# Seven block products for the mixer's last projection, memory's keys and values ahead of it, and the small-tile pool given up where the recurrences end

## The chip, the cores and the metric

The kernel runs on one core of a Trainium2 chip. Its time is the device time of one execution in microseconds; the median of several runs counts. Beside the times there is a profile of one execution: when each instruction of each engine started and how long it took, what released it when it had waited, and what the DMA queues moved. The engines are TensorE (PE in the profile; PEld is its weight load), VectorE (DVE), ScalarE (ACT), GpSimd (POOL) and SyncE (SP), which here issues DMAs.

## The reference

One layer of a streaming encoder is applied to 512 prompt tokens and 64 sample tokens, D_MODEL 1024, all in float32. After an input projection come two linear-attention recurrences in chunks of 64 tokens; their outputs are gated, projected and merged, and the merged rows go through `w_o`. That last projection, the cross-attention's keys and values and the down-projection are what the change concerns.

```python
# _mixer, its end
y_a = o_a.reshape(B, L, VA).astype(h.dtype) @ p['w_out_a'][l]
y_b = o_b.reshape(B, L, VB).astype(h.dtype) @ p['w_out_b'][l]
merged = jax.nn.sigmoid(gt_a) * y_a + jax.nn.sigmoid(gt_b) * y_b
return merged @ p['w_o'][l], conv_new, s_a_new, s_b_new

# _trunk, for the one layer (prompt and sample each)
x = x + y                                       # y = _mixer(_rmsnorm(x, norm_mix), ...)
x = x + _cross_attn(_rmsnorm(x, p['norm_mem'][l]), mem_k[l], mem_v[l], p['w_mq'][l], p['w_mo'][l])
f, f_new = _conv_ffn(_rmsnorm(x, p['norm_ffn'][l]), ...)
x = x + f                                       # then the final _rmsnorm

# keys and values of the prompt's 256 memory tokens
m = _rmsnorm(mem, g)
return (m @ w_k).reshape(B, M, MEM_HEADS, MEM_HD), (m @ w_v).reshape(B, M, MEM_HEADS, MEM_HD)

# _conv_ffn: 1024 -> 2 x 2816, causal convolution of width 3, gate, then back to 1024
return (jax.nn.silu(gate) * val) @ w_down, new
```

## The kernel before

**Layout.** Features lie on the 128 partitions, tokens in the free dimension: `x` is eight tiles of 128 x 576 (512 prompt tokens, then 64 sample tokens). A projection makes one output tile of 128 features at a time, out of eight blocks of 128 input features. Every float32 product is made of three: weight and operand are each split into a high part of type float32r and the rest, and high x high, high x low and low x high are added up in PSUM. `mm3` and `proj` (lines 621 to 653) write them out; a tile's 576 columns are done as 256 and 320, in the two banks of one `big` PSUM tile, of which there are two. Four `sm` tiles of one bank each serve the rest.

**Stages.** `main` (line 1356) goes through: the input projection's tiles with the recurrences strung in between (`c_gdn`, `c_gla`); 16 gate tiles; the `out` tiles that merge the two branches; `wo`, the last projection of the mixer, which adds into `x` and prepares the next norm (`res_finish`); then for each of four heads the memory's keys (`mk`), for every second head the values (`mv`), and the queries (`mq`), with the attention (`c_att`) strung in; the output tiles `mo`; and the FFN, whose order is written out in `ffn_order` (line 103): 22 times an up-projection pair `up`, and the down-projection in four parts of 6, 6, 6 and 4 blocks.

**Block products.** The down-projection already uses seven products in place of eight. Two output tiles are a pair, two input blocks are an even and an odd one, and the 576 tokens are two halves `N1` and `N2` of 288: a 2 x 2 by 2 x 2 block product, done with seven products of sums (P1, P2, P3, Q4 to Q7). The operand sums are `tu` and `tw` (`operands`, line 1683), the weight sums are `ws` (`emit_product`, line 515). `products` (line 1705) runs through pairs in the order of `product_order` (line 92). In a pair P1, Q6, Q7 and Q4 add up in one bank, Q5 and P3 in a second, P2 has a third; after each product VectorE adds the bank into half a tile of `x`. So a product that adds into a bank waits until VectorE has read it for the product before. All three banks were `sm` tiles.

**Weights.** `WORDER` is the one list in which weights are used. A weight is loaded by SP into one of `RAWB` = 3 raw tiles, then split by ScalarE into tiles of a ring: `WB` = 6, and in the FFN `WF` = 6 more. A projection's weight takes two tiles (high, low), a product's takes one of which it uses the two halves. `fetch` (line 562) prepares weights ahead as long as the ring has room. For most weights the low part is made by ScalarE writing the negated high part and a DMA from the POOL queue that adds the float32 weight onto it (`split_summed`, line 508).

**What sets the order.** All instructions go through `Driver` (line 196), which keeps a planned time for each engine and each tile and issues an instruction at its planned place; chains of small work (`drv.spawn`) fill in between the matmuls of `main`. TensorE's order is the order in which `main` and the chains call it. At run time each engine takes its instructions in that order and waits on semaphores only. Working tiles of 128 x 584 come from a ring of `NS` = 57 slots. Small tiles of the recurrences live in the pool `tp`; at the FFN's start it is closed and `fp`, with the six further weight tiles, takes its place:

```python
drv.flush(float("inf"))
tctx.close()
nonlocal tp, fp
tp = fp = ctx.enter_context(tc.tile_pool(name="fp", bufs=WF))
```

Of the kernel before, what the change touches and what calls it, by code (L numbers as in the profile page):

```python
# [10 lines left out]
F32 = mybir.dt.float32  # L11
# [6 lines left out]
P = 128  # L18
D = 1024
TP = 512  # L20
TS = 64
# [6 lines left out]
NS = 57  # L28
RAWB = 3
WB = 6  # L30
WF = 6
# [17 lines left out]
M_ID, M_TRI, M_NEG, M_N1, M_ONE, M_GLA, M_SH, M_LEV = 0, 128, 256, 384, 512, 640, 768, 896  # L49
# [12 lines left out]
def weight_order():  # L62
    seq = list(HEADS)
    for m in range(8):
        seq += [("gta", m), ("gtb", m)]
    seq += [("out", m) for m in range(8)]
    seq += [("wo", m) for m in range(8)]
    for hd in range(4):
        seq += [("mk", 2 * hd), ("mk", 2 * hd + 1)]
        if hd % 2 == 0:  # L70
            seq += [("mv", 2 * hd + i) for i in range(4)]
        seq += [("mq", 2 * hd), ("mq", 2 * hd + 1)]
    seq += [("mo", m) for m in range(8)]
    for kd, i in FFN:
        if kd == "up":
            seq += [("up", i), ("up", NJ + i)]
        elif kd == "dns":
            seq += [("dn*", u) for u in product_order(i)]
        else:
            seq += [("dn", (m, 3)) for m in i]  # L80
    return seq
# [6 lines left out]

PRODUCTS = ("P1", "Q5", "Q6", "P2", "P3", "Q7", "Q4")


def product_order(pairs):

    seq = []
    for i, pair in enumerate(pairs):
        seq += [(pair, "P1"), (pair, "Q5")]
        if i:
            seq.append((pairs[i - 1], "Q4"))
        seq += [(pair, p) for p in ("Q6", "P2", "P3", "Q7")]
    return seq + [(pairs[-1], "Q4")]  # L100


def ffn_order():
    seq, late = [], []
    for p, js in enumerate(PARTS):
# [4 lines left out]
        late = [("dns", [(m, p) for m in range(0, 8, 2)])]  # L110
    return seq + [("dn", (0, 1)), ("dns", [(2, 3), (4, 3)]), ("dn", (6, 7))]
# [4 lines left out]
WFULL = [w for w in WORDER if w[0] not in ("dn", "dn*")]  # L116
# [79 lines left out]
class Driver:  # L196
# [32 lines left out]
    def where(self, ap):  # L229
# [4 lines left out]
        if ap.space == bass.MemoryType.PSUM:  # L234
            return ap.tensor.name, (0, P, 0, 1024)
# [20 lines left out]
    def rotate(self, tag, bufs, tile_):  # L256
# [3 lines left out]
        if len(q) >= bufs:  # L260
            end, old = self.free_at(tag)
            q.remove(old)
# [151 lines left out]
def tile_trunk(ctx, tc, xT, memT, wt, wd, vec, cst, w0, wgate, st_gdn, st_conv, st_gla, st_ffn, ckT, cv,  # L414
# [57 lines left out]
    def raw_tile():  # L472
        return keep(drv.rotate("raw", RAWB, wp.tile([P, 1024], F32, tag="raw", name=nm("wr"), bufs=RAWB)))
# [11 lines left out]
    def emit_weight(i):  # L485
        kind, idx = WORDER[i]
        if kind == "dn*":
# [25 lines left out]
    halves_of = {}  # L513

    def emit_product(pair, prod):

        m, p = pair
        n = len(PARTS[p]) * 64
        if prod == "P1":
            r = halves_of[pair] = []  # L520
            for i in range(2):
                raw = raw_tile()
                c0 = PART0[p] * 128
                src = wd[m + i, :, c0:c0 + 2 * n]
# [5 lines left out]
        def total(a, b):  # L530
            s_ = slot("ws")
            V.tensor_tensor(s_[:, 0:n], a, b, op=ALU.add)
            r.append(s_[:, 0:n])
            return s_[:, 0:n]

        src = {"P1": lambda: a11, "Q5": lambda: total(a21, a22), "Q6": lambda: total(r[4], a11), "P3": lambda: total(r[5], a12),
               "Q7": lambda: total(a11, a21), "P2": lambda: a12, "Q4": lambda: a22}[prod]()
# [7 lines left out]
        if prod in ("P2", "Q4"):  # L545
            drop(src)
# [15 lines left out]
    def fetch(i):  # L562

        room = WB + (WF if fp is not None else 0)
        for j in range(i, len(WORDER)):
            if j in wready:
                continue
            if len(drv.pending & wnames) + (1 if WORDER[j][0] == "dn*" else 2) > room:
                break
# [11 lines left out]
    cst_t = cp.tile([P, NM], F32, name="cst")  # L581
# [12 lines left out]
    w0_t = cp.tile([P, 256], F32, name="w0")  # L594
    DMA(w0_t, w0)
    ident = cst_t[:, M_ID:M_ID + 128]
    tri = cst_t[:, M_TRI:M_TRI + 128]
    neg = cst_t[:, M_NEG:M_NEG + 128]
    negm1 = cst_t[:, M_N1:M_N1 + 128]
    ones = cst_t[:, M_ONE:M_ONE + 128]  # L600
    shift = cst_t[:, M_SH:M_SH + 128]
    glam = cst_t[:, M_GLA:M_GLA + 128]
# [8 lines left out]
    wg_t = cp.tile([P, 256], F32, name="wg")  # L611
    cst_in = cp.tile([P, 12, 3], F32, name="cstin")
    cst_out = cp.tile([P, 12, 6], F32, name="cstout")
    csamp = cp.tile([P, 12, TS], F32, name="csamp")
# [124 lines left out]
    sg = cp.tile([P, 12, 20], F32, name="sg")  # L739
# [16 lines left out]
    def c_gates(ba):  # L756
        G.memset(bt, 0.0)
        p1 = sm()
        sel = cst_t[:, M_SEL:M_SEL + 8]
# [145 lines left out]
    def c_gdn(h):  # L905
# [118 lines left out]
        for li, b in enumerate(LEVELS):  # L1024
# [10 lines left out]
            lm = cst_t[:, M_LEV + 128 * li:M_LEV + 128 * li + 128]  # L1035
# [318 lines left out]


    def main():
# [53 lines left out]
        DMA(cst_t, cst)  # L1410
# [85 lines left out]
        mem_prep()  # L1496
        yield tuple([("oa", h) for h in range(5)] + [("ob", p) for p in range(2)])
        osx = xs_of(list(zip(oh, ol)))
        mg = []
        for m in range(8):  # L1500
# [8 lines left out]
            h, lo = slot("mgh", F32R), slot("mgl", F32R)  # L1509
            A.copy(h[:, 0:T], g0[:, 0:T])  # L1510
            X.tensor_tensor(lo[:, 0:T], g0[:, 0:T], f(h[:, 0:T]), op=ALU.subtract)
            mg.append((h, lo))

        def res_finish(ps, m, scale, gcol, acc_, out):
            for xx, i in zip(two(x[m]), pv(ps)):
                V.scalar_tensor_tensor(xx, i, scale, xx, op0=ALU.mult, op1=ALU.add)
            out.append(norm_prep(x[m], vcol(gcol + m)))
            sq_acc(acc_, x[m], m == 0)

        acc = slot("acc")  # L1520
        out = []
        for m in range(8):
            xt = slot("x")
            DMA(xt[:, 0:T], xT[:, m, :])
            x[m] = xt
            b = []
            yield from tile_proj("wo", m, xs_of(mg), b)
            res_finish(b[0], m, 0.5, C_GMEM, acc, out)
        xs = xs_of(out)
        drv.spawn(c_rstat("n2", [(acc, 0)], 4, True, 2.0))  # L1530

        first = True
        yield ("nm",)
        N["mrt"], N["mbc"] = N["nm"]
        for hd in range(4):
            kr = slot("kraw")
            for j in range(2):
                wh, wl = weight("mk", 2 * hd + j)
                ps = big()
                for k in range(KT):  # L1540
                    a, b = N["mx"][k]
                    mm3([(ps[:, 0, 0:256], slice(0, 256))], wh, wl, a, b, k, k == 0, k == 7)
                    if k % 2:
                        yield 0.7
                V.tensor_tensor(kr[:, 256 * j:256 * j + 256], ps[:, 0, 0:256], N["mbc"][:, 0:256], op=ALU.mult)
            DMO(o_mk[256 * hd:256 * hd + 256, :].rearrange("(j p) t -> p j t", p=P), r4(kr[:, 0:512], 256))
            N["k", hd] = split(kr)
            ckr, cvr = slot("ckr"), slot("cvr")
            DMA(r4(ckr[:, 0:512], 256), ckT[:, 2 * hd:2 * hd + 2, :])
            DMA(r4(cvr[:, 0:512], 256), cv[:, 256 * hd:256 * hd + 256].rearrange("(a p) d -> p a d", p=P))  # L1550
            N["ks", hd], N["vs", hd] = split(ckr), cvr
            if hd % 2 == 0:
                nh = hd // 2
                vr = [slot("vraw") for _ in range(2)]
                ps = big()
                for kp in range(4):
                    wh, wl = weight("mv", nh * 4 + kp)
                    for tt in range(2):
                        c = slice(128 * tt, 128 * tt + 128)
                        for k in range(2):  # L1560
                            a, b = N["mx"][2 * kp + k]
# [427 lines left out]
```

## Time and profile before

| what | value |
|---|---|
| median of 3 runs | 1142.08 us (1141.47 to 1143.43) |
| the profiled execution | 1141.34 us, span 1139.5 us |
| TensorE busy | 1117.0 us, 8453 matmuls |
| VectorE busy | 628.7 us |
| ScalarE busy | 618.3 us |
| GpSimd busy | 294.8 us |
| HBM read / written | 163.13 MB / 5.37 MB |

A matmul's row lasts some 0.3 us, but the next one starts 0.13 us later: they are pipelined, so a matmul's cost is the distance between starts. The instructions are recorded by one helper, which is why almost all of them carry the same line, L227; they are told apart by the names of their tiles: `big<-xh,w` is a matmul into a `big` tile with operand `xh` and weight `w`. In the rows of the timeline the numbers are start and length, and in brackets at the end the idle time of the engine before it and what ended it. In the rows of stretches the numbers are the length, then for TensorE, its weight loads, VectorE, ScalarE and GpSimd the busy time and the count of instructions, then the granted clock of TensorE (1.00 is full), the mean busy share of the DMA engines and the GB/s they moved.

### The profile page before, as it was taken

Reading aid. Unit: us, or ns where it says so; the run is one execution under the profiler, and the core shown is the slowest. Engines: PE = TensorE matmul, PEld = TensorE weight load, DVE = VectorE, ACT = ScalarE, POOL = GpSimd, SP = SyncE. Lnnn points to the kernel's source line nnn. Section 1 sums busy time; section 2 is a strip of 40 time slices with the busy share of each in tenths; the row PEclk is TensorE's granted clock in tenths of the full one; section 3 lists DMA queues with packets and bytes.
Section 4 is the critical chain, followed back from the end, with each engine's and each line's share of the span. In section 5 each row is a group of like instructions: output and inputs, shape, how many; then the busy total and the mean of one; then the engine's idle time right before and its main releaser. Section 6 shows DMA issues by size and latency. Waiting matters only on the chain.

```text
span 1139.5 us, 21399 instructions
## 1 busy us (share of the span) xinstructions
PE 1117.0 (98%) x8453; PEld 1076.4 (94%) x8453; DVE 628.7 (55%) x1296; ACT 618.3 (54%) x1138; POOL 294.8 (26%) x540
## 2 busy tenths in 40 slices
PE   8999999999999999999999999899999999999997
PEld 7899989998889999999999999899999999999987
DVE  6777646555533135345563443467835773677475
ACT  6766437554534354454545555654646555656554
POOL 4244114521311131111001011324423342343332
PEclk9999999999999999999999999999999999999999
DMA  8665334654336678885836846974697579848834
GB/s 259 149 144 126 63 79 89 153 121 101 80 65 166 173 171 199 224 178 141 230 120 156 205 110 156 230 181 74 141 257 178 100 165 224 208 73 189 189 68 122
DMA packets 61557, 172.53 MB, mean 151 GB/s; under 512 B 7056, under 2 KB 19600, under 8 KB 61456
## 3 DMA queue, kind: packets, MB, share of 16 engines
q0 software_dynamic: 25632, 73.41, 37.8%
q1 hardware_dynamic: 35824, 97.74, 26.2%
q8 instruction: 67, 1.10, 0.4%
q14 instruction: 34, 0.28, 0.1%
HBM read 163.13 MB, written 5.37 MB: 148 GB/s over the span
## 4 chain that ended last, share of the span: by engine, by line
PE 93%; DVE 3%; ACT 2%; DMA 1%; issue 0%; SPq 0%; POOL 0%; ACTq 0%
PE big L227 70%; PE sm L227 22%; DMA wr<-wt 1%; ACT w L227 1%; DVE x L227 1%; DVE fc L227 0%; DVE c L227 0%; SPq L227 0%; ACT xh L227 0%; DVE acl L227 0%; ACT sq L227 0%; DVE xl L227 0%; DVE gy L227 0%; DVE w L227 0%; DVE gna L227 0%
## 5 line engine op out<-in xcount | busy, mean ns | idle before, releaser
L227 PE MATMUL big<-xh,w 128*128 128x256 f32 (+1 forms) x3072 | 554.8, 300 | 6.7 <-DMA wr<-wt 3.9
L227 PEld LDWEIGHTS big<-xh,w 128*128 128x128 f32 x3072 | 463.1, 189 | 13.1 <-issue 8.8
L227 PE MATMUL big<-xl,w 128*128 128x256 f32 (+1 forms) x1536 | 330.3, 297 | 1.8 <-DVE xl L227 1.8
L227 PEld LDWEIGHTS big<-xl,w 128*128 128x128 f32 x1536 | 259.2, 190 | 2.4 <-DVE xl L227 2.4
L227 POOL DMA_DIRECT2D w<-wt x118 | 103.3, 882 | 445.4 <-ACT w L227 411.9
L227 ACT ACTIVATE w<-wr 128x1024 fp32r<-128x1024 f32 (+3 forms) x164 | 148.6, 906 | 109.8 <-PE big L227 52.9
L227 ACT CAST w<-wr 128x1024 fp32r<-128x1024 f32 (+3 forms) x184 | 164.3, 894 | 42.7 <-issue 21.4
L227 PE MATMUL sm<-ach,w 128*128 128x288 f32 (+1 forms) x496 | 103.4, 297 | 5.4 <-DVE x L227 5.4
L227 PEld LDWEIGHTS sm<-ach,w 128*128 128x128 f32 x496 | 80.9, 188 | 7.5 <-DVE x L227 6.7
L227 DVE TENSOR_TENSOR fu<-big,rbc 128x512 f32<-128x512 f32 x88 | 36.2, 454 | 92.4 <-PE big L227 84.0
L227 DVE SCALAR_TENSOR_TENSOR fc<-fu,vec,fc 128x578 f32<-128x578 f32 x88 | 71.1, 818 | 9.7 <-ACT fc L227 9.3
L227 ACT ACTIVATE fc<-fu,vec 128x578 f32<-128x578 f32 x44 | 38.2, 871 | 68.3 <-DVE fu L227 68.3
L227 PE MATMUL sm<-acl,w 128*128 128x288 f32 (+1 forms) x248 | 68.4, 295 | 0.0
L227 POOL COPY fout<-fu 128x2 f32<-128x2 f32 x88 | 34.9, 427 | 123.4 <-DVE fu L227 123.2
L227 DVE TENSOR_TENSOR x<-x,sm 128x288 f32<-128x288 f32 (+1 forms) x100 | 43.7, 449 | 30.0 <-PE sm L227 29.8
L227 POOL DMA_DIRECT2D w<-wd x46 | 40.9, 915 | 69.0 <-ACT w L227 68.9
L227 PEld LDWEIGHTS sm<-acl,w 128*128 128x128 f32 x248 | 46.7, 188 | 0.0
L227 PE MATMUL big<-aoh,w 128*128 128x256 f32 (+1 forms) x256 | 45.1, 296 | 0.0
L227 PE MATMUL big<-oh,w 128*128 128x256 f32 (+1 forms) x256 | 44.9, 296 | 0.0
L227 PE MATMUL big<-mgh,w 128*128 128x256 f32 (+1 forms) x256 | 44.6, 295 | 0.0
L227 PEld LDWEIGHTS big<-oh,w 128*128 128x128 f32 x256 | 38.5, 188 | 0.3 <-DMA w<-wt 0.3
L227 PEld LDWEIGHTS big<-mgh,w 128*128 128x128 f32 x256 | 38.7, 189 | 0.0
(331 smaller groups left out, 1770.6 us busy)
## 6 DMA issues: line engine op xcount, KB each, us to landing
wr<-wt SPq DMA_DIRECT2D x134, 512.0 KB, 5.7
w<-wt POOLq DMA_DIRECT2D x118, 512.0 KB, 7.2
wr<-wd SPq DMA_DIRECT2D x24, 384.0 KB, 3.6
w<-wd POOLq DMA_DIRECT2D x36, 192.0 KB, 4.2
x<-xT SPq DMA_DIRECT2D x16, 288.0 KB, 6.1
w<-ws POOLq DMA_DIRECT2D x12, 192.0 KB, 4.0
wr<-wd SPq DMA_DIRECT2D x8, 256.0 KB, 3.0
o_y<-yo SPq DMA_DIRECT2D x8, 256.0 KB, 3.0
```

Source lines behind the costliest of these rows:

```text
L227: fn(*args, **kw)
```

## The change

1. **Seven products for `wo`.** The eight output tiles become four pairs, the eight input blocks four even-odd pairs. The merged tiles are no longer split as they are (`mgh`, `mgl`); for each second one a chain (`c_wo_operands`) makes the sums and their splits. `products` becomes general: the two banks a and b are now the two banks of one `big` tile, only P2's c is an `sm` tile. The order is the one of the FFN's calls (item 4), in which a pair's Q4 comes after the next pair's Q5; a second order, `whole`, is written and not used. `wo_finish` adds each product into `x`, scaled; `c_norm` prepares the norm after that.
2. **The order of the attention's front** is the list `ATT`: keys of head 0 and the first values, then `wo`, then the second values and keys 1, then queries and the remaining keys. The cached keys and values of the sample tokens are loaded with the queries.
3. **The pool swap** happens where the recurrences end, ahead of the `out` tiles. `fp` now holds three weight tiles (`WF` = 3), a fourth raw tile (`RF` = 1) and the eight tiles of `x` (`xslot`), which are loaded together after the `out` tiles; `NS` is 55. Constants that only the recurrences use move to the small-tile pool, and the constant table is loaded as two parts.
4. **The FFN's products.** The last pair of a call runs P1, Q5, Q6, P3, Q7, P2, Q4 instead of ending in P2, P3, Q7, Q4. The last pair of part 2 moves behind the last up-projection, ahead of the down tiles 0 and 1.
5. **Bookkeeping.** The planner tells PSUM banks apart (`where`); sums of weights are kept by name and a raw tile is given up when all its uses are made; `wo`'s weights are stored with even blocks first.

```diff
-NS = 57
+NS = 55
 RAWB = 3
 WB = 6
-WF = 6
+WF = 3
+RF = 1
...
-PRODUCTS = ("P1", "Q5", "Q6", "P2", "P3", "Q7", "Q4")
...
+def product_order(pairs, whole=False):
     seq = []
     for i, pair in enumerate(pairs):
-        seq += [(pair, "P1"), (pair, "Q5")]
+        last = i == len(pairs) - 1
+        now = [(pair, p) for p in (("P1", "P2", "Q5", "Q6", "Q7") if whole else
+                                   ("P1", "Q5", "Q6", "P3", "Q7", "P2", "Q4") if last else ("P1", "Q5", "Q6", "P2", "P3", "Q7"))]
         if i:
-            seq.append((pairs[i - 1], "Q4"))
-        seq += [(pair, p) for p in ("Q6", "P2", "P3", "Q7")]
-    return seq + [(pairs[-1], "Q4")]
+            now.insert(2, (pairs[i - 1], "Q4"))
+            if whole:
+                now.insert(5, (pairs[i - 1], "P3"))
+        seq += now
+    return seq + ([(pairs[-1], "P3"), (pairs[-1], "Q4")] if whole else [])
+
+WPAIRS = [(("wo", m), ("wo", m + 1)) for m in range(0, 8, 2)]
+
+ATT = [("mk", 0), ("mv", 0), ("wo", 0), ("mv", 1), ("mk", 1), ("mq", 0), ("mq", 1), ("mk", 2), ("mq", 2), ("mk", 3), ("mq", 3)]
...
-        late = [("dns", [(m, p) for m in range(0, 8, 2)])]
-    return seq + [("dn", (0, 1)), ("dns", [(2, 3), (4, 3)]), ("dn", (6, 7))]
+        pairs = [(("dn", (m, p)), ("dn", (m + 1, p))) for m in range(0, 8, 2)]
+        late = [("dns", pairs if p < 2 else pairs[:3])]
+        if p == 3:
+            seq.append(("dns", [(("dn", (6, 2)), ("dn", (7, 2)))]))
+    return seq + [("dn", (0, 1)), ("dns", [(("dn", (m, 3)), ("dn", (m + 1, 3))) for m in (2, 4)]), ("dn", (6, 7))]
...
     def raw_tile():
+        if fp is not None and (len(drv.ring.get("rawf", ())) < RF or drv.free_at("rawf") < drv.free_at("raw")):
+            return keep(drv.rotate("rawf", RF, fp.tile([P, 1024], F32, tag="rawf", name=nm("wr"), bufs=RF)))
...
+    def operands(ce, co, new=None, fe=None, fo=None):
+        u, w = slot("tu"), slot("tw")
+        V.tensor_tensor(u[:, N2], co[:, N2], ce[:, N2], op=ALU.subtract)
+        yield [u]
+        V.tensor_tensor(u[:, N1], ce[:, N1], ce[:, N2], op=ALU.subtract)
+        yield [u]
+        V.scalar_tensor_tensor(w[:, N1], u[:, N2], -1.0, ce[:, N1], op0=ALU.mult, op1=ALU.subtract)
+        yield [w]
+        V.scalar_tensor_tensor(w[:, N2], w[:, N1], -1.0, co[:, N1], op0=ALU.mult, op1=ALU.subtract)
+        if fe is None:
+            fe = hl(ce[:, N1], new)
+            yield [fe[1]]
+            fo = hl2(co, new)
+            yield [fo[1]]
+        fu = hl2(u, new)
+        yield [fu[1]]
+        fw = hl2(w, new)
...
+    def products(pairs, ops, finish, whole=False):
+        ab, cc = {}, {}
+        for pair, prod in product_order(pairs, whole):
+            if prod == "P1":
+                ab[pair] = big()
+            if prod == "P2":
+                cc[pair] = sm()
+            a, b = ab[pair][:, 0, 0:HT], ab[pair][:, 1, 0:HT]
+            c = cc[pair][:, 0:HT] if pair in cc else None
+            o = b if prod in ("Q5", "P3") else c if prod == "P2" else a
+            start = prod in ("P1", "Q5", "P2")
...
+    def swap_pools():
+        nonlocal tp, fp
+        tctx.close()
+        tp = fp = ctx.enter_context(tc.tile_pool(name="fp", bufs=WF))
+
+    def xslot(i, s="x"):
+        return drv.rotate(f"F{i}", 1, fp.tile([P, SLOT], F32R if s != "x" else F32, tag=f"F{i}", name=nm(s), bufs=1))
...
         yield tuple([("oa", h) for h in range(5)] + [("ob", p) for p in range(2)])
+        swap_pools()
...
-            h, lo = slot("mgh", F32R), slot("mgl", F32R)
-            A.copy(h[:, 0:T], g0[:, 0:T])
-            X.tensor_tensor(lo[:, 0:T], g0[:, 0:T], f(h[:, 0:T]), op=ALU.subtract)
-            mg.append((h, lo))
+            if m % 2:
+                drv.spawn(c_wo_operands(m, gates[2 * m - 2], g0))
...
+        mem_prep()
+        for m in range(8):
+            yield from out_tile(m)
+        for m in range(8):
+            x[m] = xslot(m)
+            DMA(x[m][:, 0:T], xT[:, m, :])
...
-        for m in range(8):
-            xt = slot("x")
-            DMA(xt[:, 0:T], xT[:, m, :])
-            x[m] = xt
-            b = []
-            yield from tile_proj("wo", m, xs_of(mg), b)
-            res_finish(b[0], m, 0.5, C_GMEM, acc, out)
...
+        def wo_finish(pair, prod, a, b, c):
+            m = pair[0][1]
+            xx, scale = (x[m], 0.5) if prod in ("P1", "Q6", "P3", "P2") else (x[m + 1], -0.5)
+            half = N1 if prod in ("P1", "P2", "Q4") else N2
+            V.scalar_tensor_tensor(xx[:, half], b if prod in ("Q5", "P3") else c if prod == "P2" else a, scale, xx[:, half],
+                                   op0=ALU.mult, op1=ALU.add)
+            if prod == ("P2" if m == 6 else "P3"):
+                drv.spawn(c_norm(m, C_GMEM, acc, out))
+            elif prod == "Q4":
+                drv.spawn(c_norm(m + 1, C_GMEM, acc, out))
+
+        def c_norm(m, gcol, acc_, out_):
+            yield [x[m]]
+            sq_acc(acc_, x[m], m == 0)
+            drv.done.add(("sq", m))
+            if drv.ready(*(("sq", i) for i in range(8))):
+                drv.spawn(c_rstat("n2", [(acc_, 0)], 4, True, 2.0))
+            while not drv.ready("wo"):
+                yield WAIT
+            out_.append((m, norm_prep(x[m], vcol(gcol + m))))
+            drv.done.add(("norm", gcol, m))
+
+        for kd, i in ATT:
+            if kd == "mk":
+                yield from mem_keys(i)
+            elif kd == "mv":
+                yield from mem_values(i)
+            elif kd == "wo":
+                yield tuple(("wops", m) for m in range(1, 8, 2))
+                yield from products(WPAIRS, [wops[m] for m in range(1, 8, 2)], wo_finish)
+                drv.done.add("wo")
...
-        drv.flush(float("inf"))
-        tctx.close()
-        nonlocal tp, fp
-        tp = fp = ctx.enter_context(tc.tile_pool(name="fp", bufs=WF))
```

345 lines of the change are left out of this document (173 added, 172 removed).

## The prediction

> **What bounds the kernel now.** I read the page's busy shares first, then the chain that ended last, then the waits of TensorE, then the timeline at each of those waits.
>
> ```profile
> span 1139.5 us, 21399 instructions
> PE 1117.0 (98%) x8453; PEld 1076.4 (94%) x8453; DVE 628.7 (55%) x1296; ACT 618.3 (54%) x1138; POOL 294.8 (26%) x540
> PE 93%; DVE 3%; ACT 2%; DMA 1%; issue 0%; SPq 0%; POOL 0%; ACTq 0%
> ```
>
> TensorE is busy for 98% of the span and holds 93% of the chain. Its whole idle time is 1139.5 - 1117.0 = 22.5 us, so time moves in two ways alone: fewer matmuls, or a wait of TensorE that goes or comes. The waits:
>
> ```profile
> PE sm L227 <- DVE x L227: 5.4, 9, 1.8
> PE big L227 <- DMA wr<-wt: 3.9, 1, 3.9
> PE big L227 <- DVE xl L227: 1.8, 2, 1.6
> PE big L227 <- DVE u L227: 1.7, 1, 1.7
> ```
>
> The first two are in the change's reach; the last two lie in the first 50 us, whose order of matmuls stays. The first is bank reuse among the block products (a product adds into a bank that VectorE must first have read); the second is one weight that was late.
>
> **Part 1: the products.** The last projection had 8 tiles x 8 blocks x 3 splits x 2 halves = 384 matmuls; seven products over four pairs are 4 x 7 x 4 x 3 = 336 of 288 columns, so 48 go. Their price:
>
> ```profile
> L227 PE MATMUL big<-mgh,w x256: 275/298/317, 470.9 to 521.7; 128*128 128x256 f32 x128
> 521.86 0.28 PE L227 MATMUL big<-mh,w 128*128 128x256 f32 x1
> 440.00:480.00 40.00, 40.00 (x304) 40.00 (x303) 19.04 (x37) 18.06 (x22) 6.04 (x7) 1.00 0.84 199
> 810.00:834.00 24.00, 24.00 (x183) 24.00 (x183) 15.67 (x36) 14.23 (x25) 9.73 (x14) 1.00 0.91 211
> ```
>
> The stage runs from 470.9 to 521.86, where memory's first key matmul starts: 50.96 / 384 = 0.1327 us each (256 and 320 columns in turn). The two windows' columns are engine busy time and count: 40.00 / 304 = 0.1316 us in the projections, 24.00 / 183 = 0.1311 us in the FFN's existing products of 288 columns, so the new shape costs no more each. 48 x 0.1327 = **-6.4 us**, on TensorE and so on the path.
>
> What the products add elsewhere, in a stage of 336 x 0.1327 = 44.6 us:
>
> ```profile
> L227 DVE TENSOR_TENSOR ws<-ws,wr 128x384 f32<-128x384 f32 x24 | 13.3, 552 | 0.1
> L227 DVE TENSOR_TENSOR aol<-sm,aoh 128x512 fp32r<-128x512 f32 x8 | 5.5, 692 | 22.0 <-ACT aoh L227 22.0
> L227 DVE TENSOR_TENSOR x<-x,sm 128x288 f32<-128x288 f32 x98 | 43.1, 451 | 30.0 <-PE sm L227 29.8
> L227 DVE TENSOR_TENSOR acc<-acc,sq 128x576 f32<-128x576 f32 x23 | 17.3, 754 | 1.4 <-ACT sq L227 1.0
> L227 ACT CAST w<-wr 128x512 fp32r<-128x512 f32 x8 | 4.9, 610 | 0.6 <-DMA wr<-wt 0.5
> ```
>
> VectorE: 16 weight sums and 12 low parts of 512 columns at 0.69 (between the 0.552 of 384 columns and 0.754 of 576; the row of that width says 0.692), 28 adds into x at 0.45, seven square sums at 0.75: 11.0 + 8.3 + 12.6 + 5.3 = 37.2 us, 83% of the stage, against 65% (15.67 of 24.00) in the FFN's products. ScalarE: 28 casts and 16 negated copies at 0.61, 26.8 us or 60%, and eight squares on top. Both fit, so they cost nothing as throughput; what is dear is lateness, next.
>
> ```profile
> 834.67 0.56 PE L227 MATMUL sm<-ach,w 128*128 128x288 f32 x3
> 835.77 0.40 PE L227 MATMUL sm<-ach,w 128*128 128x288 f32 x1 [0.55 <-DVE x L227]
> 807.61 0.40 PE L227 MATMUL sm<-ach,w 128*128 128x288 f32 x1 [0.40 <-DVE x L227]
> ```
>
> At 834.67 the third matmul starts 2 x 0.13 later, 834.93; the next was due at 835.06 and came at 835.77, and its successor follows 0.24 instead of 0.13 behind. A product right behind another in its bank thus loses 0.82 us: the idle figure of 0.55 plus 0.27 of refilling. In the new stage none stands so. The closest distance is one product of 12 matmuls, 1.58 us, for Q6 behind P1 in the first pair and all through the last; elsewhere two or more lie between. Against it stand 0.84 (0.71 + 0.13) plus whatever is ahead on VectorE: at 807.61, in a call's first pair, even two products between did not do, and 0.7 was lost (0.58 late, 0.11 refilling). Bounds: 0 if VectorE is free each time, 0.82 for each of the 28 products, 23 us, if never. I take one such wait in the first pair, where VectorE still makes the last operands, and 0.3 in the last: **+1.0**, near the lower end because the FFN's 98 products, most of them shorter (9 matmuls, 1.18 us), met only nine waits.
>
> **Part 2: the pool swap.** Before, small tiles gave way to six weight tiles at the FFN's start:
>
> ```profile
> 724.46 0.51 PE L227 MATMUL big<-xh,w 128*128 128x256 f32 x2 [3.91 <-DMA wr<-wt]
> 720.00:730.00 10.00, 6.09 (x35) 5.88 (x34) 5.83 (x11) 7.07 (x10) 2.41 (x9) 0.83 1.05 274
> 725.00:730.00 5.00, 5.00 (x28) 5.00 (x27) 4.28 (x7) 3.83 (x6) 1.12 (x5) 0.66 1.05 274
> 800.00:840.00 40.00, 39.05 (x294) 38.59 (x293) 26.21 (x57) 23.75 (x41) 14.28 (x20) 1.00 0.82 190
> ```
>
> The DMA engines are full (1.05), the weight comes late, TensorE idles 3.91 us and then runs at a granted clock of 0.66 for five microseconds. In ten microseconds 35 matmuls were done where the 304-in-40 rate does 76: 41 x 0.132 = **-5.4 us** if the wait goes. I take all of it: after the change up to four weights instead of three stand ready there, and no pool changes hands. [...]
>
> The swap now comes where the recurrences end. TensorE's instruction order is the same up to the last output matmul, with weights for two output tiles, 12.7 us of work, already loaded; x is fetched there in eight loads. Nothing at the swap costs TensorE in my sum; if the cover is gone, it is the 5.4 again (a rival).
>
> **Part 3: the order of the FFN's products.** The last pair of each call now puts P2 between Q7 and Q4, one product of 1.18 us against 0.84. Three calls lost 0.82 and the last 0.91 (1118.53 for a matmul due at 1117.73, plus 0.11):
>
> ```profile
> 1117.47 0.42 PE L227 MATMUL sm<-ach,w 128*128 128x288 f32 x2
> 1118.53 0.38 PE L227 MATMUL sm<-ach,w 128*128 128x288 f32 x1 [0.64 <-DVE x L227]
> ```
>
> 3 x 0.82 + 0.91 = **-3.4**. The first pair's wait at 807.61 (0.7, three times) keeps its order: 0. At the FFN's end one pair of part 2, 63 matmuls or 8.3 us, now stands between the last up-projection and the down tiles 0 and 1, which waited for it:
>
> ```profile
> 1102.65 0.53 PE L227 MATMUL big<-ach,w 128*128 128x256 f32 x2 [0.40 <-ACT ach L227]
> 1103.44 0.54 PE L227 MATMUL big<-acl,w 128*128 128x256 f32 x2 [0.26 <-DVE acl L227]
> 1106.19 0.43 PE L227 MATMUL sm<-ach,w 128*128 128x288 f32 x2
> 1108.39 0.40 PE L227 MATMUL sm<-ach,w 128*128 128x288 f32 x1 [1.77 <-DVE x L227]
> 1110.47 0.41 PE L227 MATMUL sm<-ach,w 128*128 128x288 f32 x1 [0.22 <-DVE x L227]
> ```
>
> The first two lost about 1.0 (their idle time and 0.2 of refilling each); 1108.39 was due at 1106.45 (1.94 + 0.11), 1110.47 lost 0.5: 3.5 in all. But VectorE does the last gate's work while that pair asks for its reads one product apart: I put two waits of 0.7 there, and 0.4 for products that now take a bank pair that the down tiles use just before. -3.5 + 1.4 + 0.4 = **-1.7**; bounds -3.5 and +2.
>
> **Part 4: memory's keys and values.** The same matmuls in another order. The first keys and values cover the making of the last operands; the second pair covers the norm (eight VectorE steps of 0.92 behind eight of ScalarE):
>
> ```profile
> L227 DVE SCALAR_TENSOR_TENSOR xl<-x,vec,xh 128x576 fp32r<-128x576 f32 x24 | 21.8, 920 | 16.1 <-ACT xh L227 16.1
> 531.75 0.39 PE L227 MATMUL big<-w,mh 128*128 128x512 f32 x1
> 540.87 0.42 PE L227 MATMUL big<-xh,w 128*128 128x256 f32 x2
> ```
>
> One call of each lasts from 521.86 to 540.87, 19.0 us with the few matmuls strung in (a value's matmul stands at 531.75), against 7.4 us of norm steps: 0, and a late statistic would cost at most the 1 to 2 us between them and the chain's end.
>
> **Weights.** Nine weight tiles instead of twelve in the FFN. Before, the rows of one late-prepared product:
>
> ```profile
> 806.58 1.75 POOL L227 DMA_DIRECT2D w<-wd  x2 [2.45 <-ACT w L227]
> 818.41 0.30 PE L227 MATMUL sm<-hl,w 128*128 128x288 f32 x1
> w<-wd POOLq DMA_DIRECT2D x36, 192.0 KB, 4.2
> ```
>
> Issued by 808.3 at the latest and landed 4.2 later, 812.5, for use at 818.41: 5.9 us in hand. Three tiles fewer take 3 x 1.18 = 3.5, and 2.4 are left: 0.
>
> **The sum.** -6.4 + 1.0 - 5.4 - 3.4 - 1.7 = -15.9 against the profiled execution's 1141.34, which stands 0.7 below the median of 1142.08: 1125.4 there, 1126 as a median.
>
> **Rivals.**
>
> ```profile
> x<-xT SPq DMA_DIRECT2D x16, 288.0 KB, 6.1
> mem<-memT SPq DMA_DIRECT2D x4, 256.0 KB, 8.7
> ```
>
> (a) *The late weight moves along with the swap*: memory's four loads and x's eight, 1.0 and 2.3 MB, meet the weights, and TensorE waits once behind the swap. For it: the full DMA engines at 720. Against: 12.7 us of weights in hand. 5.4 is given back: 1131.5. (b) *VectorE's lateness takes the products' gain*: at 83% it makes half of the 28 products wait 0.82, 11.5 instead of my 1.0: 1136.5. For it: waits at 807 with VectorE fully packed; against: VectorE stood idle 29.8 us ahead of the 98 adds quoted above, waiting for TensorE. (c) *Slower: nine tiles are too few.* If the 5.9 us in hand are not typical, the four of seven products whose low part is completed by a POOL-issued transfer come late, 48 of the FFN's 84; each by 0.33 us eats the 15.9, and by 0.5 us it is 24: 1150. For it: 2.4 us is thin; against: no weight was late in those stages. [...] Here such a transfer still landed in 4.2 us with VectorE at 65%, so I give it little. (d) *Every wait in reach goes and none comes*: -6.4 - 5.4 - 3.4 - 3.5 = -18.7: 1123.
>
> **How the numbers follow.** My forecast (1124 to 1129) 0.53, (a) 0.12, (b) 0.10, (d) 0.10, (c) 0.07; 0.08 for gains eaten by several causes, of which 0.03 within 0.2%, 0.05 above. 0.2%, 2.3 us, is about what a measurement here can tell from no change. Faster 0.85, same 0.03, slower 0.12. The range reaches from (d) with 2 us of slack, 1121, past (b), to 1140.
>
> **What would show it.** Right: the last projection's stage lasts 45 to 47 us; no DMA wait near the FFN's start and a clock of 1.00 there; waits of products on x under 5 us in all; TensorE busy near 1108. Wrong: a wait above 3 us behind the swap (a); many waits of 0.5 in the last projection (b); waits for weights inside the FFN's products (c).

## The result, and the profile after

The changed kernel takes 1155.17 us (median of 4 runs, 1152.18 to 1155.66) against 1141.78 for the kernel before on the same chip: a ratio of 1.0109, 95% interval 1.0089 to 1.0129. It is slower by about 13 us where the prediction said 16 us faster. The profiled execution took 1155.36 us, its span is 1153.6, which is 14.1 us more than the 1139.5 of before.

From the page of the changed kernel, its span and its busy shares:

```profile
span 1153.6 us, 21398 instructions
PE 1116.7 (97%) x8405; PEld 1069.4 (93%) x8405; DVE 665.4 (58%) x1354; ACT 630.2 (55%) x1174; POOL 300.7 (26%) x554
```

The 48 matmuls are gone (8405 for 8453), and TensorE is as busy as before: 1116.7 for 1117.0 us. Here the busy figure did not fall with the count, because TensorE is held up in a way that its idle time shows only in part (0.55 of 0.82 us in the rows further down), so the next view is its waits (in all, times, longest; the helper that records all operations now stands at line 239):

```profile
PE big L239 <- DVE x L239: 17.8, 32, 1.0
...
PE big L239 <- DMA w<-wt: 1.8, 1, 1.8
...
PE big L239 <- ACT vraw L239: 1.7, 3, 0.6
```

Waits on `x`, that is on VectorE's read of a bank, were 5.4 us at 9 places and are 17.8 at 32. The loading wait of 3.9 at the FFN's start is gone; new are one of 1.8 for a weight, three of 0.6 on `vraw`, and one of 1.4 for a weight in the last products. The stretches of the last projection and of the first FFN call, first of the kernel before, then of the changed kernel, and after them the changed kernel's FFN start, in the form of the prediction's rows (length, busy time and count of TensorE, its weight loads, VectorE, ScalarE, GpSimd, then granted clock, DMA share, GB/s):

```profile
470.87:521.86 50.99, 50.99 (x387) 50.99 (x385) 20.12 (x33) 25.14 (x30) 5.29 (x7) 1.00 0.77 184
802.28:837.06 34.78, 33.84 (x254) 33.37 (x253) 23.86 (x52) 20.90 (x37) 13.42 (x19) 1.00 0.85 196
```

```profile
492.04:542.69 50.65, 46.54 (x338) 44.77 (x337) 34.73 (x61) 32.04 (x55) 11.27 (x13) 1.00 0.78 193
802.22:841.38 39.16, 35.33 (x254) 33.70 (x253) 25.64 (x55) 21.95 (x41) 14.98 (x22) 1.00 0.83 188
720.00:730.00 10.00, 10.00 (x74) 9.59 (x74) 5.00 (x10) 5.07 (x7) 2.92 (x10) 1.00 0.61 127
725.00:730.00 5.00, 5.00 (x40) 5.00 (x39) 3.53 (x6) 3.51 (x5) 1.94 (x5) 1.00 0.62 148
```

The last projection lasts 50.65 us with 336 matmuls; before it was 50.99 with 384. The FFN's first call lasts 39.16 us; before it was 34.78 with the same 252 matmuls. (A stretch also counts the last few matmuls of the work ahead of it.) At the FFN's start the clock is 1.00 and TensorE never idle: that part came as forecast.

What such a wait looks like, VectorE and TensorE in the first call, around P1 and Q5 of the first pair:

```profile
803.42 0.30 PE L239 MATMUL big<-ach,w 128*128 128x288 f32 x1
803.55 0.29 PE L239 MATMUL big<-acl,w 128*128 128x288 f32 x1
803.69 0.29 PE L239 MATMUL big<-ach,w 128*128 128x288 f32 x1
...
804.02 0.46 DVE L239 TENSOR_TENSOR x<-x,big 128x288 f32<-128x288 f32 x1
...
804.53 0.40 PE L239 MATMUL big<-acl,w 128*128 128x288 f32 x1 [0.55 <-DVE x L239]
...
804.77 0.30 PE L239 MATMUL big<-ach,w 128*128 128x288 f32 x1
```

The three matmuls on top belong to Q5, which adds into bank b. VectorE is to read P1's result, which lies in bank a. Yet VectorE's read begins only when Q5's third matmul has ended (803.69 + 0.29), and Q5's fourth begins only when the read has ended (804.02 + 0.46). Between starts lie 0.84 us and then 0.24 in place of twice 0.13: 0.82 us lost, the very price that the prediction read off for two products in *one* bank. Only 0.55 of it shows as idle time; the other 0.27 counts as busy: 0.16 is the rest of the third matmul's row (0.29 long, where starts are 0.13 apart), 0.11 the longer distance behind the fourth (0.24 for 0.13). At 23 waits more than before that is 6.2 us (an estimate from these rows), as much as the 48 x 0.13 that the matmuls left out take off: so the busy time did not fall. Gaps of this size stand at seven places of the call, 5.7 us in all: in Q5 of the first and the last pair (the read of P1), in Q6 of the second (that of Q5), in P3 of the second, third and last (that of Q6) and in Q7 of the last (that of P3). Each time one half of the tile is written while the other is to be read; at three of the places another product lies between the two. Elsewhere it is the read that stands back. P1 of the second pair, its last three matmuls, and its read:

```profile
811.02 0.57 PE L239 MATMUL big<-hl,w 128*128 128x288 f32 x3
...
812.82 0.46 DVE L239 TENSOR_TENSOR x<-x,big 128x288 f32<-128x288 f32 x1 [0.57 <-PE big L239]
```

P1 has ended at 811.59; VectorE reads it 1.2 us later, the last 0.57 us of them without work, when the whole of Q5 has ended in the other half. So the reads run late, and meet products further on.

### The profile page after: what moved, and what is told of

The parts are those of the page before. It is cut to its first block, busy times and chain, and to the rows that moved or that the text cites. A ratio compares the mean times of both kernels' runs of the same rounds, so it can differ in the third digit from the quotient of the medians.

```text
span 1153.6 us, 21398 instructions
## 1 busy us (share of the span) xinstructions
PE 1116.7 (97%) x8405; PEld 1069.4 (93%) x8405; DVE 665.4 (58%) x1354; ACT 630.2 (55%) x1174; POOL 300.7 (26%) x554
## 4 chain that ended last, share of the span: by engine, by line
PE 93%; DVE 3%; DMA 2%; issue 1%; ACT 1%; SPq 0%; POOL 0%; POOLq 0%; ACTq 0%; DVEq 0%
PE big L239 77%; PE sm L239 16%; DVE x L239 1%; DMA w<-wt 1%; DMA x<-xT 1%; DMA mem<-memT 0%; DVE c L239 0%; SPq L239 0%; DVE xl L239 0%; DVE xi L239 0%; DVE gy L239 0%; DVE gna L239 0%; ACT vraw L239 0%; ACT gx L239 0%; ACT mh L239 0%
## 5 line engine op out<-in xcount | busy, mean ns | idle before, releaser
L239 POOL DMA_DIRECT2D w<-wt x122 | 107.2, 878 | 404.0 <-ACT w L239 327.3
L239 PE MATMUL big<-ach,w 128*128 128x288 f32 (+1 forms) x624 | 132.9, 298 | 11.7 <-DVE x L239 9.6
L239 PEld LDWEIGHTS big<-ach,w 128*128 128x128 f32 x624 | 102.1, 188 | 16.3 <-DVE x L239 10.1
L239 PE MATMUL big<-acl,w 128*128 128x288 f32 (+2 forms) x312 | 86.4, 299 | 8.2 <-DVE x L239 8.2
L239 DVE TENSOR_TENSOR fu<-big,rbc 128x512 f32<-128x512 f32 (+1 forms) x88 | 36.3, 453 | 77.0 <-PE big L239 74.0
L239 PEld LDWEIGHTS big<-acl,w 128*128 128x128 f32 x312 | 58.3, 188 | 11.7 <-DVE x L239 11.7
L239 POOL COPY fout<-fu 128x2 f32<-128x2 f32 x88 | 28.8, 360 | 154.0 <-DVE fu L239 154.0
L239 DVE TENSOR_TENSOR x<-x,big 128x288 f32<-128x288 f32 (+2 forms) x92 | 39.7, 448 | 38.4 <-PE big L239 37.8
L239 ACT CAST w<-ws 128x384 fp32r<-128x384 f32 (+2 forms) x72 | 36.3, 519 | 29.6 <-DVE ws L239 25.3
L239 DVE TENSOR_TENSOR gt<-big,rbc 128x512 f32<-128x512 f32 (+1 forms) x32 | 13.2, 451 | 45.7 <-PE big L239 45.7
```

The lines of the kernel that those rows point to most:

```text
L239: fn(*args, **kw)
```

## The experiments

Theory 1: reads and writes are ordered by tile, not by bank. The changed kernel made banks a and b two halves of one tile, so products in different banks of a pair wait as if they shared one. Theory 2: VectorE or the nine weight tiles are too slow for the products (the prediction's rivals (b) and (c)). Theory 3: the loss lies in the new order of memory's work and the swap.

**Separate tiles again.** In the changed kernel, a and b become `sm` tiles taken when first used, as before:

```diff
-            if prod == "P1":
-                ab[pair] = big()
-            if prod == "P2":
-                cc[pair] = sm()
-            a, b = ab[pair][:, 0, 0:HT], ab[pair][:, 1, 0:HT]
+            bank = pair, "b" if prod in ("Q5", "P3") else "c" if prod == "P2" else "a"
+            start = bank not in banks
+            if start:
+                banks[bank] = sm()
+            o = banks[bank][:, 0:HT]
...
```

> The changed kernel, with the banks a and b of a pair of products as two small tiles instead of the two halves of one tile; nothing else differs. Theory 1 (a product that writes one half waits for VectorE's read of the other half, because waits go by tile; P1 before Q5 and P3 before Q7, back to back, lose some 0.6 us each): the last projection's stage falls from 50.65 to 45-46 us, the FFN's calls of 252 matmuls from 39.16 to 34-35, and the whole to 1128-1138 us. Theory 2 (the products are late because VectorE is too loaded or the weights are too few): the stages stay within 1 us and the whole stays at 1150-1157. Theory 3 (the cores of the loss are the new order of memory's work and the swap): the products stay as they are, 1150-1157, and waits named x stay above 15 us.

Measured: 1132.31 us (1129.96 to 1133.70), ratio to before 0.9913 (0.9899 to 0.9928), 22.9 us less than the changed kernel. The same two stretches of products:

```profile
490.59:535.89 45.30, 45.20 (x338) 44.61 (x336) 34.52 (x61) 31.95 (x55) 11.31 (x13) 1.00 0.87 213
795.70:829.33 33.63, 33.63 (x254) 33.40 (x253) 25.23 (x55) 22.05 (x41) 14.68 (x22) 1.00 0.88 196
```

VectorE and ScalarE do the same work in them (34.52 for 34.73 us, 31.95 for 32.04), and TensorE is not held up: 45.30 for 50.65 and 33.63 for 39.16. The place of the rows above, P1's last matmul on top:

```profile
796.76 0.29 PE L239 MATMUL sm<-hl,w 128*128 128x288 f32 x1
796.90 0.29 PE L239 MATMUL sm<-ach,w 128*128 128x288 f32 x1
...
797.30 0.30 PE L239 MATMUL sm<-acl,w 128*128 128x288 f32 x1
...
797.30 0.45 DVE L239 TENSOR_TENSOR x<-x,sm 128x288 f32<-128x288 f32 x1
797.43 0.30 PE L239 MATMUL sm<-ach,w 128*128 128x288 f32 x1
...
797.56 0.29 PE L239 MATMUL sm<-acl,w 128*128 128x288 f32 x1
```

While VectorE reads one bank (797.30 to 797.75), TensorE starts a matmul into another every 0.13 us. VectorE's read lasts 0.45 us here and 0.46 with the shared tile. So the loss shows no contention in PSUM; it is a wait that came with the shared tile and went with it. That the program orders its reads and writes by tile is inferred from this pair of runs and from where the waits begin and end. The products changed banks in the changed kernel too; starts 0.13 us apart through VectorE's read of another bank came only with tiles of their own. Theories 2 and 3 are refuted as causes of these 22.9 us. The longest waits on other things that are left here:

```profile
PE big L239 <- DVE u L239: 1.7, 1, 1.7
PE big L239 <- ACT vraw L239: 1.7, 3, 0.6
PE big L239 <- DMA w<-wt: 1.7, 1, 1.7
```

**The shared tile alone.** In the kernel before, only the banks of a pair are put into one `big` tile, and the planner tells its halves apart, as in the changed kernel:

```diff
+                if prod == "P1":
+                    ab[pair] = big()
                 if start:
-                    banks[bank] = sm()
+                    banks[bank] = sm() if prod == "P2" else ab[pair][:, "ab".index(bank[1]), :]
...
-            return ap.tensor.name, (0, P, 0, 1024)
+            return ap.tensor.name, (0, P, lo // 512 * 512, (hi + 511) // 512 * 512)
```

> The kernel before, with only this of the change: the banks a and b of a pair are the two halves of one tile, and the planner counts reads and writes of such a tile by half. Order of products, weights, pools, last projection as before. Theory 1: P1 before Q5 and P3 before Q7 lose some 0.6 us each, 9 places in a call of four pairs; 14 to 17 us in all: 1152-1160 us, and the calls of 252 matmuls last 39-40 us instead of 34.8. Theories 2 and 3: within 3 us of before, 1139-1145.

Measured: 1176.11 us (1174.43 to 1177.77), ratio 1.0297 (1.0282 to 1.0311). The waits on `x`, and the FFN's first call:

```profile
PE big L227 <- DVE x L227: 24.7, 41, 2.3
```

```profile
805.88:849.48 43.60, 36.73 (x254) 33.77 (x253) 24.55 (x52) 21.79 (x38) 13.32 (x19) 1.00 0.76 172
```

This part of the change alone makes before slower by 34 us. The direction was as theory 1 had it, the size was not: I had spread the loss over the places and taken 0.6 for each of nine places in a call. In this call twelve gaps between matmuls cost 0.82 to 0.88 us each and one 0.4, 10.3 in all; the call of before had 1.5 of such waits, so that 8.8 come on top, the measured 43.60 - 34.78. In the changed kernel's order the same tile cost seven gaps. Another 2.6 us of the 34 lie in the attention's front (126.6 for 124.0), with three waits on memory's values, told below, since the planner's line reaches them too.

**A planner that knows.** In the changed kernel, only the planner's line goes back, so that it counts the tile as one thing; the tile stays shared:

```diff
-            return ap.tensor.name, (0, P, lo // 512 * 512, (hi + 511) // 512 * 512)
+            return ap.tensor.name, (0, P, 0, 1024)
```

> The changed kernel, with only the planner told that a tile of two halves is one thing again (the tile itself is still one). Theory 1 (the wait is the tile's, whoever plans it): the waits stay, 1148-1160 us. Rival (the planner, which does not know of the wait, puts VectorE's read in a bad place; a planner that knows removes it): 1128-1140 us.

Measured: 1170.96 us (1168.75 to 1173.36), ratio 1.0252 (1.0235 to 1.0269): above what either expected, and slower than the changed kernel. Its TensorE and VectorE in the second pair of the first call:

```profile
812.83 1.35 PE L239 MATMUL big<-hl,w 128*128 128x288 f32 x9
814.82 0.37 PE L239 MATMUL big<-ach,w 128*128 128x288 f32 x1 [0.64 <-DVE x L239]
```

```profile
814.22 0.45 DVE L239 TENSOR_TENSOR x<-x,big 128x288 f32<-128x288 f32 x1 [0.27 <-PE big L239]
814.59 1.15 DVE L239 TENSOR_TENSOR ws<-ws,wr 128x384 f32<-128x384 f32 x2
```

The wait now sits between P1 and Q5 instead of inside Q5; P1's nine matmuls have ended, at 814.18, when VectorE reads, at 814.22. It costs 0.88 us here (0.93 and 0.21 between starts for twice 0.13). The call has seven such places, two of about 1.0 and one of 1.7. Planning moved the wait here and did not remove it.

**The new order of the FFN's products alone**, in the kernel before, with small tiles:

```diff
-        seq += [(pair, p) for p in ("Q6", "P2", "P3", "Q7")]
+        seq += [(pair, p) for p in (("Q6", "P3", "Q7", "P2") if i == len(pairs) - 1 else ("Q6", "P2", "P3", "Q7"))]
...
-        late = [("dns", [(m, p) for m in range(0, 8, 2)])]
+        late = [("dns", [(m, p) for m in range(0, 8 if p < 2 else 6, 2)])]
+        if p == 3:
+            seq.append(("dns", [(6, 2)]))
```

> The kernel before, with only the new order of the FFN's products: P2 between Q7 and Q4 in the last pair of each call, and one pair of the third part kept back to stand between the last up-projection and the down tiles; banks stay small tiles. The prediction's Part 3 put this at -3.4 and -1.7: 1136-1138 us. If VectorE's lateness at the end eats it: 1140-1144.

Measured: 1143.06 us (1139.93 to 1143.81), ratio 1.0005 (0.9996 to 1.0013): no gain. Three calls of it, two of 252 matmuls and one of 189, and VectorE at the start of the second:

```profile
802.93:836.91 33.98, 33.59 (x255) 33.35 (x253) 23.83 (x52) 21.23 (x37) 13.46 (x20) 1.00 0.86 200
913.15:949.34 36.19, 34.47 (x255) 33.58 (x254) 25.44 (x55) 21.42 (x37) 12.36 (x19) 1.00 0.82 187
1025.57:1053.25 27.68, 26.00 (x192) 25.15 (x190) 19.21 (x41) 16.78 (x26) 9.04 (x13) 1.00 0.78 185
```

```profile
914.46 0.75 DVE L229 TENSOR_TENSOR acl<-tu,ach 128x576 fp32r<-128x576 f32 x1
915.17 0.82 DVE L229 SCALAR_TENSOR_TENSOR fc<-fu,vec,fc 128x578 f32<-128x578 f32 x1
915.91 0.75 DVE L229 TENSOR_TENSOR acl<-tw,ach 128x576 fp32r<-128x576 f32 x1
916.58 0.44 DVE L229 TENSOR_TENSOR x<-x,sm 128x288 f32<-128x288 f32 x1
```

The first call is 0.8 us shorter, as Part 3 of the prediction had it, and the wait at the end of each call is gone. But the second is 1.4 us longer: here the low parts of the last operands and a convolution step stand ahead of VectorE's read of P1 (916.58), and the third product waits 1.0 us for it. In before, VectorE reads P1 1.6 us after the call's start and only then does the convolution step; here it is 3.4 us. What was won at a call's end was lost at the next one's start; why the planner puts the step first here is not shown. The third call is 1.5 us longer than three quarters of before's 34.90. In the kernel with separate tiles the calls with the same order last 33.63 and 33.71: the wait of 0.8 at the end is gone, and the one of 0.7 at the start is 0.3. So the order is worth 0.8 us a call where VectorE's start is not disturbed.

**Values, the same wait on ScalarE.** Separate tiles, and the planner's line taken back as above. With the products in small tiles this touches only tiles read half by half, memory's values above all, where ScalarE empties one half while TensorE writes the other. The rows of the changed kernel, ScalarE and then TensorE:

```profile
490.24 0.47 ACT L239 ACTIVATE vraw<-big,rt 128x256 f32<-128x256 f32 x1 [1.35 <-PE big L239]
```

```profile
489.81 0.39 PE L239 MATMUL big<-w,mh 128*128 128x512 f32 x1
490.76 0.51 PE L239 MATMUL big<-w,mh 128*128 128x512 f32 x1 [0.56 <-ACT vraw L239]
```

> The separate banks of e1_split_banks, and the planner counts a tile of two halves as one thing again, which now touches only tiles that are read half by half: memory's values above all, where ScalarE reads the first half while TensorE still writes the second. Theory 1 (the three waits named vraw, 0.56 us idle and about 0.8 us each with the refilling, are the same wait by tile): they go, and the attention's front (from the first key matmul to the first mo matmul, without the products) falls by 2 to 2.5 us: 1129-1131 us. Rival (ScalarE is late there whatever the planner knows): 1131-1134.

Measured: 1129.18 us (1126.82 to 1129.95), ratio 0.9883 (0.9865 to 0.9900). No wait on `vraw` is left, and the attention's front without the products falls from 126.30 to 123.86 us (17.65 + 108.65 and 16.81 + 107.05, from starts of matmuls): the same 0.8 us three times. Its remaining late weights, at the second output tile and in the last products:

```profile
436.00 0.53 PE L239 MATMUL big<-oh,w 128*128 128x256 f32 x2 [2.01 <-DMA w<-wt]
...
1100.22 0.66 PE L239 MATMUL sm<-ach,w 128*128 128x288 f32 x3 [1.04 <-DMA w<-ws]
1101.88 0.67 PE L239 MATMUL sm<-ach,w 128*128 128x288 f32 x3 [0.60 <-DMA w<-wd]
1104.95 0.37 PE L239 MATMUL sm<-ach,w 128*128 128x288 f32 x1 [0.95 <-ACT w L239]
```

**The number of weight tiles**, on that kernel, one up and one down:

```diff
-WF = 3
+WF = 4
```

> e5_values_too with ten weight tiles behind the swap instead of nine. If tiles are too few at the FFN's end (waits of TensorE for w of 1.3, 0.4 and 0.9 us in the last six products), they shrink: 1.5 to 3.5 us less than e5_values_too. If VectorE and ScalarE set the weights' time there, no change within 0.7.

Measured: 1125.95 us (1123.48 to 1127.26), ratio 0.9856 (0.9840 to 0.9872), 3.2 below the nine tiles. The two intervals overlap a little (nine tiles: 0.9865 to 0.9900); the traces bear the gain out, since the three waits for `w` in the last products are gone and these take 12.73 us for 14.96. The last projection is 1.2 us longer (46.65 for 45.43), with a new wait of 0.6 for a weight.

```diff
-WF = 3
+WF = 2
```

> e5_values_too with eight weight tiles behind the swap instead of nine: the price of one tile, for the prediction's rival (c). By the prediction's own sum (2.4 us in hand with nine, 1.2 us a tile) nothing is late in the FFN's calls yet: within 1.5 us of e5_values_too. If nine is already the edge: 5 us or more above it, with waits for w in the calls of 252 matmuls.

Measured: 1134.08 us (1132.49 to 1134.45), ratio 0.9928 (0.9915 to 0.9940), 4.9 above the nine tiles: far outside the 1.5 of the first expectation and at the edge of the second. The wait that grows most is not the one for `w`:

```profile
PE sm L239 <- DVE x L239: 4.2, 4, 1.1
```

Its first call lasts 35.83 us (34.04 with nine tiles, 33.35 with ten). VectorE at the start of that call, which begins at 792.67:

```profile
793.61 0.45 DVE L239 SCALAR_TENSOR_TENSOR tw<-tw,fc 128x288 f32<-128x288 f32 x1
793.98 0.75 DVE L239 TENSOR_TENSOR acl<-tu,ach 128x576 fp32r<-128x576 f32 x1
794.70 0.82 DVE L239 SCALAR_TENSOR_TENSOR fc<-fu,vec,fc 128x578 f32<-128x578 f32 x1
795.43 0.75 DVE L239 TENSOR_TENSOR acl<-tw,ach 128x576 fp32r<-128x576 f32 x1
796.10 0.45 DVE L239 TENSOR_TENSOR x<-x,sm 128x288 f32<-128x288 f32 x1
```

The same late read of P1 as under the new order in before: the last operands' low parts and a convolution step stand ahead of it, and it starts 3.4 us into the call. With nine tiles it starts after 1.6, the step behind it. No sum of weights stands ahead of the read in either, so one tile fewer cost time mostly through another planned order on VectorE; how the count of tiles brings that order about is not shown. Waits for weights stand in the products too, 0.5 us in the first call and 0.8 in the last products at the longest. Nine was not too few in the sense of rival (c), but it was not free.

**The swap.** With nine tiles, memory's loading and splitting moved back ahead of the swap; then the same with ten tiles; then, in addition, the extra raw buffer used only later:

```diff
+        mem_prep()
         yield tuple([("oa", h) for h in range(5)] + [("ob", p) for p in range(2)])
         swap_pools()
...
-        mem_prep()
...
-        if fp is not None and (len(drv.ring.get("rawf", ())) < RF or drv.free_at("rawf") < drv.free_at("raw")):
+        if fp is not None and wpos[0] > WORDER.index(("out", 3)) and (len(drv.ring.get("rawf", ())) < RF or drv.free_at("rawf") < drv.free_at("raw")):
```

> e5_values_too with the loading and splitting of memory put ahead of the wait for the recurrences and of the pool swap, where the kernel before had it. If memory's four loads are what makes the second output weight late behind the swap (1.7 us, rival (a) in small), the output stage falls from 53.2 to about 51.8 us and the whole by 1.5 against e5_values_too. If the nine-tile burst of weight loads at the swap does it alone, the wait stays: within 0.5 of e5_values_too.

> Ten weight tiles and memory's loading ahead of the swap together. If the two gains add (3.2 and about 0.5 us below e5_values_too): 1124.5-1126. If memory's work ahead of the swap only shifts the late output weight: the same as e7_ten_tiles, 1125-1127.

> e9_ten_early, and the extra buffer for raw weights behind the swap is used only from the fourth output weight on. Theory: the first load into it stands in SyncE's queue until the small tiles' last reader is done, and the loads behind it wait too (no transfer at all for 3 to 5 us ahead of the swap); used later, the wait of 1.2 to 1.7 us at the second output weight goes: the output stage 51.5-52 us, 1123-1124.5 in all. Rival (the burst of weight loads, or the adds on GpSimd ahead of a weight's transfer, make it late): the wait stays, within 0.7 of e9_ten_early.

Measured: 1128.63 (1127.72 to 1130.10), 1126.14 (1125.26 to 1126.86) and 1126.08 us (1125.20 to 1127.62); ratios 0.9883, 0.9859 and 0.9863, each with an interval of about 0.0015 to either side. The wait at the second output weight in the three:

```profile
434.92 0.53 PE L239 MATMUL big<-oh,w 128*128 128x256 f32 x2 [1.19 <-DMA w<-wt]
```

```profile
435.09 0.53 PE L239 MATMUL big<-oh,w 128*128 128x256 f32 x2 [1.44 <-DMA w<-wt]
```

```profile
433.62 0.53 PE L239 MATMUL big<-oh,w 128*128 128x256 f32 x2 [0.31 <-DMA w<-wt]
```

Moving memory takes 0.8 off the wait (2.01 to 1.19 us) and leaves the rest. Using the extra raw buffer later brings it to 0.31, and the output stage from 53.05 to 51.91 us, which was 51.78 before. So, by one profile each, most of the wait hung on when that buffer is used. That the loads behind it stood in SyncE's queue was the theory; transfers still pause ahead of the swap in this run (0 GB/s from 413.5 to 416.0 us; with ten tiles alone from 415.0 to 418.0), so that way is not shown. In the times neither step is resolved: memory's move changed 1129.18 to 1128.63 and 1125.95 to 1126.14, and the 1123 to 1124.5 expected of the last kernel did not come. Ten tiles against nine is clear over the five kernels, 1126.0 to 1126.1 in three and 1128.6 and 1129.2 in two. The fastest kernels of the study are thus the last three with ten tiles, about 1126 us: 16 us below before, 29 below the changed kernel.

## Why the prediction was wrong

Terms against the stretches between starts of matmuls (us, difference to before; the whole spans differ by +14.1 and -10.1, of which the rows leave 0.2 and 0.5):

| term | predicted | changed kernel | with separate tiles |
|---|---|---|---|
| the last projection | -6.4 + 1.0 | -0.3 | -5.7 |
| FFN's start (swap) | -5.4 | -5.6 | -5.4 |
| second output weight | 0 | +1.7 | +1.5 |
| attention's front | 0 | +2.2 | +2.3 |
| FFN's first two calls | -0.8 each | +4.4 each | -1.1 each |
| FFN from its third call to the end | -3.4 | +5.4 | -1.6 |
| ahead of the output stage | 0 | +1.9 | +0.6 |

- *Part 1, "In the new stage none stands so."* This is the step that failed. It counted the distance between products by bank, though the change's own text said that a and b are the two banks of one tile. The same step had the right price, 0.82 us for a product behind another, and in (b), "half of the 28 products wait 0.82", a rival of the right form, but put its cause in VectorE's load. Eight waits stand in the stage, seven of 0.82 to 0.88 and one of 0.3, 6.2 us in all where the sum had 1.0; VectorE, 34.73 us busy for an estimated 37.2, was no hindrance.
- *Part 3, "keeps its order: 0"* and the two gains of the new order failed for the same reason: seven places of a call now wait, and most of the loss lies here. By itself the order brought nothing in before (1.0005), 0.8 us a call with separate tiles, as forecast. From the third call to the end the forecast of -3.4 was met only with a tenth tile as well (-4.5; -1.6 with nine). The wait at a call's start was taken as fixed at 0.7, and it varies with what stands ahead of the read on VectorE: 0.3 us in the first call with separate tiles, over 2 in the second call of before with the new order (an estimate: it lasts 36.19 us, 2.2 more than the first with its 33.98).
- *Part 2* held: -5.6 us for -5.4, clock 1.00, no wait. "Nothing at the swap costs TensorE" was wrong by 1.7 us: rival (a), with its place right and its price a third.
- *Part 4*, 0, was wrong by 2.2 us, three waits of the same kind on ScalarE, brought by the planner's line and not by the new order; with that line back the front stands at 123.86 us for 123.98 before.
- *Weights: "2.4 are left: 0"* was too good: 3.2 us by the run with ten tiles. The last products, where waits of 1.04, 0.60 and 0.95 for `w` stood, account for 2.2 of them.
- Of the 29 us between forecast and result, 22.9 come back with separate tiles, 3.1 with the planner's line and 3.2 with a tenth weight tile. The time forecast, 1126 us, is what the change gives once these three are there. That the number is met in the end says little: the forecast had not seen the tile, and it had put memory, weights and the second output weight at nothing.

The rise ahead of the output stage is mostly the spread of executions, as far as the profiles show. In the ten kernels of the experiments that stage starts at 419.2 to 421.3 us, which takes in the changed kernel's 420.9; in the two built on before, whose work up to there is that of before, it starts 0.8 us later than in the profile of before. Whether the change has a part in it stays open.

## What to carry to other kernels

What ordered two engines here, by the pair of runs with a shared tile and with separate ones (1155.17 and 1132.31 us), is the unit in which the program tracks its buffers. Banks that alternate between a writer and a reader belong into tiles of their own; two halves of one tile cost 0.8 us at each of some thirty places here (32 waits on `x` in the changed kernel, most of 0.55 us idle). When a change re-allocates a buffer that one engine fills while another empties it, count the neighbours by tile and not by bank, and look at what it does to every other user of that kind of tile. If a count of matmuls falls and TensorE's busy time does not (8453 to 8405 here, with 1117.0 and 1116.7 us), look for waits in the middle of an accumulation.

## What the runs showed that was not expected

A wait in the middle of a product cost as much here as one at its start in the kernel before: 0.82 us for a read of 0.46, since the read began only when the last matmul started had ended (0.29 us from its start to its end), and TensorE's next start came 0.24 us before the one after it in place of 0.13. It goes both ways: VectorE's read also stood behind matmuls that wrote a bank it did not read, 1.2 us in the rows above, 0.57 of them idle. And a planner that knew of the shared tile made it dearer, 0.88 us and more, at more places (43 waits on `x` for 32), 1170.96 us for 1155.17.
